# A late store in six parts instead of four, and the last store whole

## The chip, the cores and the metric

The kernel runs on one core of one Trainium2 chip. The metric is the device time of one execution in microseconds (us); the figure given for a kernel is the median of its runs.

## The reference

Eight batches of twelve heads, each with Q, K and V of 512 rows by 64 columns in float32. The softmax is over a 64 x 64 matrix of each head (attention between columns), and V is multiplied by it:

```python
Q_norm = Q / (np.linalg.norm(Q, axis=-2, keepdims=True) + 1e-10)
K_norm = K / (np.linalg.norm(K, axis=-2, keepdims=True) + 1e-10)
attn = np.einsum('bhnd,bhne->bhde', Q_norm, K_norm)
attn = np.exp(attn - np.max(attn, axis=-1, keepdims=True))
attn = attn / (np.sum(attn, axis=-1, keepdims=True) + 1e-10)
return np.einsum('bhnd,bhde->bhne', V, attn).astype(np.float32)
```

Q, K and V together are 37.75 MB to read, and the output is 12.58 MB to write.

## The kernel before

The 96 heads go in 24 units (`U`) of four heads, and two units make one of 12 steps (`S`). For a unit, Q and K are cast to bf16 side by side (`cast_qk`), and `grams` multiplies the pair by itself, so that one 128 x 128 matrix of a head holds the squares of the norms on its diagonal and Q against K off it. `squares`, `sums` and `powers` make the scales, `scale_k`, `logits`, `exps` and `normalise` the softmax, whose result stands as a block-diagonal `ab`. V goes in six groups (`W`): cast (`cast_v`), transposed on TensorE (`vtrans`), copied out of PSUM (`vcopy`) and multiplied by `ab` (`outs`). `ocopy` brings each of four outputs `x` of a step into an SBUF tile `so[s, i]`, two of them (halves of its rows) to a tile, and `store(s, i)` writes the tile to the output.

A tile `so[s, i]` has 128 partitions; in each lie two rows `r` of 2 KB, and the two rows go to different places of the output. A whole store is therefore 512 KB in 256 pieces of 2 KB. There are 24 stores, `(0, 0)` to `(11, 1)`, all issued from SP's queue. There are 13 `so` buffers.

The order of everything is worked out by a planner (`Order`): each piece of work has a cost on an engine, what must have ended before it, what it must follow, and a rank; for a store the rank is `v_at(...) + ST_LAG`, which puts most stores behind the loads. The planner's result is written out engine by engine. At the end of SP's queue stand, in this order, the rest of the loads, fourteen whole stores, the store `FEW = (S - 3, 1)`, which is `(9, 1)`, the stores `(10, 0)`, `(10, 1)`, `(11, 0)`, and the last one, `(11, 1)`, as two pieces of the planner, `sh` and `st`.

`store` treats two of these specially. For `FEW` it issues four DMAs: row 0 of partitions 0 to 91, of 92 to 95 and of 96 to 127 (L204), and then row 1 of all 128 partitions (L205). The two pieces of `(11, 1)` each take the half of the columns that one `ocopy` has written (`rows`, L207), so that a DMA has 256 pieces of 1 KB.

The DMAs use eight completion semaphores in turn: the one that is issued as the ninth has the semaphore of the first, and waits on SP until that first has landed in full.

Of the kernel before, what the change touches and what calls it, by code (L numbers as in the profile page):

```python
# [16 lines left out]
J = T // 2  # L17
# [85 lines left out]
def kernel(  # L103
# [7 lines left out]
    nc = tc.nc  # L111
# [3 lines left out]
    S = U // 2  # L115
# [46 lines left out]
    qk32, v32, vb, qkb, gram, scr, kq, n2, r8, kqs, rq, lg, ex, ab, vps, vt, po, so = ({} for _ in range(18))  # L162
# [32 lines left out]
        else:  # L195
            nc.sync.dma_start(out=o[:, c], in_=i[:, c])

    def store(s, i, k=None):
        rows = slice(None) if k is None else slice(k * (J // 2), (k + 1) * (J // 2))
        o = Of[s // 2, s % 2, i].rearrange("p r (j d) -> p r j d", d=D)  # L200
        if (s, i) == FEW:

            for a, b in ((0, 92), (92, 96), (96, 128)):
                nc.sync.dma_start(out=o[a:b, 0], in_=so[s, i][a:b, 0])  # L204
            nc.sync.dma_start(out=o[:, 1], in_=so[s, i][:, 1])  # L205
            return
        nc.sync.dma_start(out=o[:, :, rows], in_=so[s, i][:, :, rows])  # L207

    def cast_qk(u, x):
        s, r = divmod(u, 2)  # L210
# [137 lines left out]
    for i in range(NB["ab"]):  # L348
        a = const.tile([128, HU, 2 * D], BF16, name=f"ab{i}")
# [9 lines left out]
    X = 1.29  # L359
    R = dict(cq=2.5, gr=2.471, sq=0.756, kq=1, rd=3.457, pw=3.5, sc=1, rq=1.9, lg=5, ex=1.1, nm=2.545, cv=1.165, vt=0.9, vc=1.1, ou=2, oc=0.9)  # L360
    BIAS = dict(sc=-0.6, kq=5, cv=1, vc=-0.3, oc=0.6)
    QK_PACE, V_FROM, V_PACE, ST_LAG = 0.631, 0.0377, 0.7486, 1.5133

    def v_at(v):
        return V_FROM + V_PACE * v / U

    def piece(key, engines, after, behind, rank, fn, *args):
        if key[0] in ("cv", "vc", "oc", "kq", "sc"):
            plan.add(key, engines, after, behind, rank, lambda eng: fn(eng, *args))
        else:  # L370
            plan.add(key, engines, after, behind, rank, lambda eng: fn(*args))

    def back(kind, i, n, *rest):
        return (kind, i - n, *rest) if i - n >= 0 else None
# [17 lines left out]
    for u in range(U):  # L392
        s, r = divmod(u, 2)
# [17 lines left out]
    def turns(w):  # L411
        return [(q, f) for q in range(4) for f in ((0, 1) if w == W - 1 and q >= TAIL else (None,))]
# [29 lines left out]
    for s in range(S):  # L442
        for x in range(4):
            i, k = divmod(x, 2)
            n = 4 * s + x - 2
            wait = [("oc", n // 4, n % 4)] if n >= 0 else []
            order = [("ou", s, x - 1) if x else back("ou", s, 1, 3)]
            piece(("ou", s, x), {"PE": 0.5}, [("vc", s // 2, *t) for t in turns(s // 2) if t[0] // 2 == k] + [("nm", s)] + wait, order, R["ou"] + 0.01 * s, outs, s, x)
            n = 2 * s + i - NB["so"]
            free = [("st", n // 2, n % 2)] if k == 0 and n >= 0 else []  # L450
            order = [("oc", s, x - 1) if x else back("oc", s, 1, 3)]
            piece(("oc", s, x), {"ACT": 0.6, "DVE": (0.68, BIAS["oc"])} if s >= BOTH else {"ACT": 0.6}, [("ou", s, x)] + free, order, R["oc"] + 0.01 * s, ocopy, s, x)
        for i in range(2):
            order = [("st", s, 0) if i else back("st", s, 1, 1)]
            if (s, i) == (S - 1, 1):

                piece(("sh", s, i), {"DMA": 0.67}, [("oc", s, 2)], order, v_at(2 * s + i) + ST_LAG, store, s, i, 0)
                piece(("st", s, i), {"DMA": 0.67}, [("oc", s, 3)], [("sh", s, i)], v_at(2 * s + i) + ST_LAG, store, s, i, 1)
            else:
                piece(("st", s, i), {"DMA": X}, [("oc", s, 2 * i), ("oc", s, 2 * i + 1)], order, v_at(2 * s + i) + ST_LAG, store, s, i)  # L460

    ahead = [loaded(x, 0, r) for r in range(2) for x in range(2)]
    held, passed = [], False
# [40 lines left out]
```

## Time and profile before

| | us |
|---|---|
| median of 3 runs | 128.76 (128.62 to 128.79) |
| span of the profiled execution, first to last instruction | 127.0 |
| around the span, if that execution took the median time (no time of its own is listed for it) | 1.76 |
| DMA queue of SP (q1): share of 16 engines' span | 96.4% |
| DVE busy | 92.8 (73%) |
| TensorE busy | 77.7 (61%) |
| ACT busy | 72.5 (57%) |
| POOL busy | 36.6 (29%) |
| last copy into `so` (ACT, second of two from 114.00) ends | 115.1 |

A DMA runs on up to 16 DMA engines, and the profile's DMA share is the mean busy share of all 16; packets overlap a little, so that a share of 1.04 to 1.06 stands for all of them at work. "To landing" is the time from a DMA's issue until its semaphore has the last of its updates. The trace also records each update of a semaphore by a DMA, one for every DMA engine that carried a part of it: sixteen for most DMAs. These are called landings below. Times within the execution are in us from the start of its span.

### The profile page before, as it was taken

The numbers are of one execution on the slowest core, as the hardware profiler recorded it, in microseconds if no ns is written. First come the engines' busy times: TensorE is split into PE (matmuls) and PEld (weight loads), VectorE is DVE, ScalarE is ACT, GpSimd is POOL, SyncE is SP. The second block draws the span as 40 slices with busy tenths as digits, with TensorE's granted clock in tenths as the row PEclk, the third lists the DMA queues.
The fourth block names the chain that finished last, engine by engine and source line by source line (L and its number), as shares of the span: only waits on it lengthen the run. The fifth ranks groups of instructions, "written<-read, shape, count | busy, mean of one in ns | idle before, by whom it ended". The sixth has DMA issues, their size and how long they took to land.

```text
span 127.0 us, 4887 instructions
## 1 busy us (share of the span) xinstructions
PE 77.7 (61%) x2128; PEld 62.9 (50%) x2128; DVE 92.8 (73%) x141; ACT 72.5 (57%) x220; POOL 36.6 (29%) x40
## 2 busy tenths in 40 slices
PE   0065384894844679858594879566797869680000
PEld 0054372773633568647482668445585748460000
DVE  3354749859899899999885898999999799820000
ACT  4000441569877077786692786794829969972000
POOL 4006307300906903033065212213453361200000
PEclk9999999999998555999958967998559995955555
DMA  4999999999999999999999999999999999999993
GB/s 114 415 434 410 430 410 418 417 437 403 425 426 415 410 419 421 405 415 426 430 410 413 415 421 427 412 419 428 401 413 410 403 402 406 401 405 408 405 366 106
DMA packets 15629, 50.64 MB, mean 399 GB/s; under 512 B 1144, under 2 KB 1656, under 8 KB 14200
## 3 DMA queue, kind: packets, MB, share of 16 engines
q1 hardware_dynamic: 15320, 49.29, 96.4%
q10 hardware_dynamic: 288, 1.05, 2.1%
q8 instruction: 16, 0.26, 0.7%
q14 instruction: 5, 0.04, 0.1%
HBM read 37.75 MB, written 12.58 MB: 396 GB/s over the span
## 4 chain that ended last, share of the span: by engine, by line
DVE 39%; DMA 21%; PE 13%; ACT 11%; issue 4%; POOL 2%; DVEq 0%; SPq 0%; POOLq 0%; ACTq 0%
DMA qk<-in_Q_dram 21%; DVE qkb L213 15%; PE gram L233 9%; DVE scr L240 7%; DVE ab L291 6%; ACT vt L166 4%; DVE vb L168 4%; ACT ex L282 3%; ACT so L166 3%; PE vps L302 3%; DVE n L252 2%; DVE vt L168 2%; DVE so L168 2%; PE po L319 1%; ACT kq L166 1%
## 5 line engine op out<-in xcount | busy, mean ns | idle before, releaser
L233 PE MATMUL gram<-qkb 32*128 32x128 bf16 (+1 forms) x1504 | 35.5, 257 | 23.1 <-DVE qkb L213 9.9
L233 PEld LDWEIGHTS <-qkb 32*128 32x128 bf16 (+1 forms) x1504 | 29.9, 114 | 27.7 <-DVE qkb L213 12.7
L213 DVE CAST qkb<-qk 128x1024 bf16<-128x1024 f32 x48 | 36.4, 780 | 8.5 <-DMA qk<-in_Q_dram 6.9
L170 POOL TENSOR_SCALAR vb<-v 128x1024 bf16<-128x1024 f32 x19 | 21.2, 1129 | 45.5 <-DMA v<-in_V_dram 32.0
L166 ACT COPY so<-po 128x512 f32<-128x512 f32 x45 | 25.0, 593 | 5.2 <-PE po L319 5.0
L166 ACT COPY vt<-vps 128x1024 bf16<-128x1024 bf16 (+1 forms) x18 | 17.8, 989 | 17.4 <-PE vps L302 17.3
L302 PE MATMUL vps<-identb,vb 128*128 128x128 bf16 x192 | 20.2, 262 | 5.8 <-POOL vb L170 3.7
L319 PE MATMUL po<-ab,vt 128*64 128x128 bf16 x384 | 19.3, 242 | 5.2 <-issue 2.7
L263 POOL TENSOR_TENSOR kqs<-kq,r 64x512 f32<-64x512 f32 x12 | 14.0, 1164 | 25.8 <-ACT r L259 13.4
L240 DVE SCALAR_TENSOR_TENSOR scr<-gram,eye 64x512 f32<-64x512 f32 x24 | 16.5, 687 | 4.4 <-PE gram L233 4.1
L302 PEld LDWEIGHTS <-vb 128*128 128x128 bf16 x192 | 14.7, 117 | 10.0 <-POOL vb L170 5.1
L319 PEld LDWEIGHTS <-vt 128*64 128x64 bf16 x384 | 13.8, 121 | 9.2 <-issue 4.6
L282 ACT ACTIVATE ex<-lg,rq 128x64 f32<-128x64 f32 x48 | 14.5, 322 | 2.8 <-PE lg L276 2.7
L166 ACT COPY kq<-gram 64x512 f32<-64x512 f32 x12 | 7.0, 581 | 13.5 <-DVE scr L240 13.4
L291 DVE TENSOR_TENSOR ab<-ex,rinv 64x256 bf16<-64x256 f32 x24 | 13.9, 579 | 0.6
L282 ACT ACTIVATION_READ_ACCUMULATOR ex<-lg,rq 128x1 f32 x48 | 10.2, 213 | 0.0
L168 DVE CAST vb<-v 128x1024 bf16<-128x1024 f32 x5 | 7.6, 1527 | 1.2 <-DMA v<-in_V_dram 1.2
L252 DVE TENSOR_REDUCE n<-scr 128x8 f32<-128x512 f32 x12 | 8.1, 679 | 0.1
L276 PE MATMUL lg<-eye,kqs 64*128 64x64 f32 x48 | 6.4, 259 | 2.6 <-issue 1.5
L168 DVE COPY vt<-vps 128x1024 bf16<-128x1024 bf16 (+1 forms) x8 | 7.9, 1019 | 0.1
L276 PEld LDWEIGHTS lg<-eye,kqs 64*128 64x128 f32 x48 | 4.5, 156 | 4.4 <-issue 2.0
L288 DVE RECIPROCAL rinv<-esum 128x4 f32<-128x4 f32 x12 | 2.1, 171 | 2.8 <-ACT ex L282 2.8
(17 smaller groups left out, 16.0 us busy)
## 6 DMA issues: line engine op xcount, KB each, us to landing
v<-in_V_dram SPq DMA_DIRECT2D x11, 1024.0 KB, 17.1
out_dram<-so SPq DMA_DIRECT2D x22, 512.0 KB, 10.2
qk<-in_Q_dram SPq DMA_DIRECT2D x8, 1024.0 KB, 17.4
qk<-in_K_dram SPq DMA_DIRECT2D x8, 1024.0 KB, 17.1
qk<-in_Q_dram SPq DMA_DIRECT2D x8, 512.0 KB, 12.2
qk<-in_K_dram SPq DMA_DIRECT2D x6, 512.0 KB, 12.5
qk<-in_K_dram ACTq DMA_DIRECT2D x2, 512.0 KB, 7.3
v<-in_V_dram SPq DMA_DIRECT2D x2, 512.0 KB
```

The costliest lines, as they stand in the source:

```text
L166: nc.scalar.copy(o, i)
L168: nc.vector.tensor_copy(o, i)
L170: nc.gpsimd.tensor_scalar(out=o, in0=i, scalar1=1.0, scalar2=0.0, op0=ALU.mult, op1=ALU.add)
L213: nc.vector.tensor_copy(qkb[u][:, :, x * D:(x + 1) * D], qk32[s][:, x, r])
L233: nc.tensor.matmul(gram[s][:, h, r, 0], x, x, start=(t == 0), stop=(t == (T if u < WIDE else J) - 1))
L240: nc.vector.scalar_tensor_tensor(out=scr[s][half], in0=gram[s][half, :, :, 0, half].rearrange("p h r d -> p (h r) d"), scalar=1e-20, in1=e ...
L263: (nc.vector if eng == "DVE" else nc.gpsimd).tensor_tensor(out=kqs[s][HI], in0=kq[s][HI], in1=r8[s][HI, :, None].to_broadcast([D, 2 * HU, ...
L276: nc.tensor.transpose(l[:, h, :], kqs[s][HI, 2 * h:2 * h + 2].rearrange("p r d -> p (r d)"), eye2[HI])
L282: nc.scalar.activation(e[:, h, :], lg[s][:, h, :], AF.Exp, scale=rq[s][:, h:h + 1], accum_out=z[:, h:h + 1])
L291: nc.vector.tensor_tensor(out=a[half, :, half], in0=e[half], in1=ri[half, :, None].to_broadcast([D, HU, D]), op=ALU.mult,)
L302: nc.tensor.transpose(ps[:, c, n, :], vb[w][:, J * c + j].rearrange("p r d -> p (r d)"), identb)
L319: nc.tensor.matmul(po[s, x][e * D:(e + 1) * D, j].rearrange("p r d -> p (r d)"), v, ab[s][:, h, :])
```

## The change

Row 1 of the store `FEW` leaves in the same three parts as row 0, so that the store is six DMAs instead of four. The last store `(11, 1)` is one DMA with pieces of 2 KB instead of two with pieces of 1 KB, and the planner's special pieces for it go. The instructions of the other engines and their order are the same as before, and so is SP up to this store; SP has one DMA more in all (L204 six times, and L206 for the whole stores).

```diff
-    def store(s, i, k=None):
-        rows = slice(None) if k is None else slice(k * (J // 2), (k + 1) * (J // 2))
+    def store(s, i):
         o = Of[s // 2, s % 2, i].rearrange("p r (j d) -> p r j d", d=D)
         if (s, i) == FEW:
-            for a, b in ((0, 92), (92, 96), (96, 128)):
-                nc.sync.dma_start(out=o[a:b, 0], in_=so[s, i][a:b, 0])
-            nc.sync.dma_start(out=o[:, 1], in_=so[s, i][:, 1])
+            for r in range(2):
+                for a, b in ((0, 92), (92, 96), (96, 128)):
+                    nc.sync.dma_start(out=o[a:b, r], in_=so[s, i][a:b, r])
             return
-        nc.sync.dma_start(out=o[:, :, rows], in_=so[s, i][:, :, rows])
+        nc.sync.dma_start(out=o, in_=so[s, i])
...
-            if (s, i) == (S - 1, 1):
-                piece(("sh", s, i), {"DMA": 0.67}, [("oc", s, 2)], order, v_at(2 * s + i) + ST_LAG, store, s, i, 0)
-                piece(("st", s, i), {"DMA": 0.67}, [("oc", s, 3)], [("sh", s, i)], v_at(2 * s + i) + ST_LAG, store, s, i, 1)
-            else:
-                piece(("st", s, i), {"DMA": X}, [("oc", s, 2 * i), ("oc", s, 2 * i + 1)], order, v_at(2 * s + i) + ST_LAG, store, s, i)
+            piece(("st", s, i), {"DMA": X}, [("oc", s, 2 * i), ("oc", s, 2 * i + 1)], order, v_at(2 * s + i) + ST_LAG, store, s, i)
```

## The prediction

> **What bounds the kernel now.** First the table of stretches at the end of the span (columns: length, busy time of each engine, granted clock, DMA share of 16 engines, GB/s).
>
> ```profile
> 110.00:116.00 6.00, 3.32 (x62) 2.53 (x56) 1.71 (x4) 4.40 (x13) 0.00 (x0) 0.64 1.05 406
> 116.00:120.00 4.00, 0.00 (x0) 0.00 (x0) 0.00 (x0) 0.00 (x0) 0.00 (x0) 0.50 1.05 405
> 120.00:122.00 2.00, 0.00 (x0) 0.00 (x0) 0.00 (x0) 0.00 (x0) 0.00 (x0) 0.50 1.06 407
> 122.00:123.00 1.00, 0.00 (x0) 0.00 (x0) 0.00 (x0) 0.00 (x0) 0.00 (x0) 0.50 0.92 353
> 123.00:124.00 1.00, 0.00 (x0) 0.00 (x0) 0.00 (x0) 0.00 (x0) 0.00 (x0) 0.50 0.83 307
> 124.00:125.00 1.00, 0.00 (x0) 0.00 (x0) 0.00 (x0) 0.00 (x0) 0.00 (x0) 0.50 0.73 258
> 125.00:125.50 0.50, 0.00 (x0) 0.00 (x0) 0.00 (x0) 0.00 (x0) 0.00 (x0) 0.50 0.12 41
> 125.50:126.00 0.50, 0.00 (x0) 0.00 (x0) 0.00 (x0) 0.00 (x0) 0.00 (x0) 0.50 0.03 10
> 126.00:127.00 1.00, 0.00 (x0) 0.00 (x0) 0.00 (x0) 0.00 (x0) 0.00 (x0) 0.50 0.00 0
> ```
>
> After 116 no compute engine does anything. Only stores move, at 405 GB/s until 122, and then the rate falls in steps: DMA engines run out of work one after another. From 125.5 to 126 a share of 0.03 is 0.03 x 16 x 0.5 = 0.24 us of one engine's time: one engine alone is still at work. So the end is set by the DMA engine with most left to do, not by compute (the last copy into `so` ended at 115.1) and not by the mean of the engines.
>
> Next, SP's issues in time and what SP waited for (from 96 on): the stores are issued one by one as earlier ones land, eight back.
>
> ```profile
> 110.63 2.80 SPq L204 DMA_DIRECT2D out_dram<-so  x3
> 114.40 0.37 SPq L205 DMA_DIRECT2D out_dram<-so  x1
> 115.75 4.76 SPq L207 DMA_DIRECT2D out_dram<-so  x5
> ```
> ```profile
> SPq L207 <- DMA out_dram<-so: 6.8, 10, 0.9
> SPq L204 <- DMA out_dram<-so: 2.5, 3, 1.0
> ```
>
> Then the issues with their time to landing. The first four rows are of the store `FEW`, the last two of stretches that hold a whole store `(10, 0)` to `(11, 0)` and the first half of `(11, 1)`.
>
> ```profile
> out_dram<-so SPq DMA_DIRECT2D x1, 184.0 KB
> out_dram<-so SPq DMA_DIRECT2D x1, 8.0 KB
> out_dram<-so SPq DMA_DIRECT2D x1, 64.0 KB, 7.2
> out_dram<-so SPq DMA_DIRECT2D x1, 256.0 KB, 6.4
> ```
> ```profile
> out_dram<-so SPq DMA_DIRECT2D x1, 512.0 KB, 6.4
> out_dram<-so SPq DMA_DIRECT2D x1, 256.0 KB, 5.8
> ```
>
> The rows of 184 and 8 KB have no time to landing, and the landings tell why: each has four updates by DMA engines, where all others have sixteen. The part of 92 partitions landed at 118.70, 118.95, 119.30 and 119.94, that of 4 at 118.88, 119.12, 119.48 and 120.12: each 0.18 after the other, so the same four engines, which I call the four. The store before it landed on them at 116.85, 117.10, 117.44 and 118.09 (the four of its sixteen landings that the part of 92 follows by the same 1.85); 92 partitions on four engines are 23 pieces of 2 KB for each, 1.85 / 23 = 0.080 us a piece. Eight of the other twelve were late before it, at 119.11 to 119.52; four were early, 116.44 to 118.09. A whole store gives each engine 16 pieces, and the landings of two such follow at 1.27 to 1.30, again 0.080 a piece. The next DMAs keep the order: the slowest of the four is at 120.30 after the part of 32 partitions (113.1 + 7.2), 120.83 after the whole row (114.40 + 6.4), 122.12 after `(10, 0)` (115.75 + 6.4), then 123.41, 124.68, 125.37 (first half of the last store, 119.58 + 5.8) and 126.05, the last landing of all. The last half landed on the other fifteen at 122.48 to 125.54: 122.48, 122.69, 123.03 and 124.0 on the early four, the rest within 0.7 of each other. After 126.05 come 0.93 us of semaphore and drain work of the end.
>
> **The change part by part.**
> *Row 1 of `FEW` in three parts.* Before, each engine gets 8 pieces of it. After, each of the four gets 23 + 1 + 2 = 26 and each of the other twelve 2 (32 partitions over 16 engines). For the four that is 18 more: 18 x 0.080 = +1.45 us; for the twelve 6 fewer: -0.48 us. Price of the two extra DMAs on an engine: the slowest of the four had 1 + 2 + 8 pieces in three DMAs from 119.94 to 120.83, 0.89 / 11 = 0.081 a piece, so a DMA more costs next to nothing there (at most 11 x 0.001 = 0.01 us).
> *SP.* One DMA more in all, about 0.3 us of issue time (2.80 us are three of L204 and the waits between; the longest alone is 0.34), hidden, since SP is waiting between all of these. But each DMA takes one of the eight semaphores. The six parts wait for whole stores eight back, which landed at 110.57 and then every 1.28: issues at 110.6, 111.8, 113.1, 114.4, 115.7 and 117.0; `(10, 0)` at 118.25, 2.5 later than before, `(10, 1)` at 119.55, `(11, 0)` when the first part of 92 has landed (120.0), `(11, 1)` when the first part of 4 has (120.12) and SP is free (120.5). The four have work until after 122 and don't notice. The twelve have only 2 + 2 pieces between the store before `FEW` and `(10, 0)`. From issue to first packet it was 1.0 us at the start (Q's first load, issued 0.74, first packet 1.75), and at most 1.5 in this tail, where each next piece followed the last without a gap. So `(10, 0)` can start at 119.3 to 119.8. The eight late ones are through with the earlier pieces at 119.5 to 119.9: a gap of 0 to 0.3 us. The early four stand still for up to 1 us. This moves only engines with slack, as follows.
> *The last store whole.* Pieces of 2 KB in place of twice as many of 1 KB. Two halves took 0.69 + 0.69 on the slowest engine (124.68 to 126.05), a whole store 1.27 (123.41 to 124.68): -0.10 us on every engine. The wait for the last `ocopy` is no cost: it ended at 115.1, the issue is at 120.5, and the slowest engine gets to it at about 126.1. If that cover were gone, the cost would be the 0.5 us between the end of the two last copies; it is not.
> *Compute.* No instruction is moved on PE, DVE, ACT or POOL, and nobody waits for these stores: the tiles of `(9, 1)` to `(11, 1)` are not written again. Cost 0.
>
> **The sum.** Slowest of the four: 126.05 + 1.45 - 0.10 = 127.40. Slowest of the twelve: 125.54 - 0.48 - 0.10 + (0 to 0.3) = 125.0 to 125.3. The four are the last, so the end moves by 127.40 - 126.05 = +1.35 us. From the profiled span: 127.0 + 1.35 = 128.35. The median of the runs is 128.76, 1.76 over that span; with that unchanged, 130.1 us.
>
> One rule is to be weighed against these rows. The landings show four engines for the parts of 92 and 4 partitions. The Trainium skill, "DMA: Bandwidth & Descriptors", section "Why a DMA increments its semaphore by 16 and not by 1", has the number of engines as the largest up to 16 that divides the slowest dimension, and for such DMAs the lowest-numbered engines; 92 gives 4, as the trace has it, so the second part of 92 would meet the same four engines, and the sum is the +1.35 above. [...]
>
> **The rivals.** A measurement of this kernel can tell about 0.2% (0.26 us) from no change.
> *The four are not the last engines in an unprofiled run.* One trace shows that they are last, 126.05 against 125.54; the order could differ from run to run. If the slowest of the four is x us ahead of the slowest of the twelve, the gain is 0.58 on the twelve and the end moves by 1.35 - x, until x = 1.93. At x = 0.5: 129.6; at x = 1: 129.1. For: the page has 16 fetches of instructions with 0.7% of 16 engines' span, 0.007 x 16 x 127 / 16 = 0.9 us each, and one of them on another engine would change the order. Against: three runs within 0.17 us.
> *Faster:* the same with x over 1.93: the twelve decide, and -0.58 gives 128.2; it is faster by over 0.26 from x = 1.61 on. For: the twelve do shed 6 pieces each. Against: it needs a lag of over 2.1 us from what the trace shows.
> *The second part of 92 goes to other engines.* The early four could take +1.45 (their 124.0 becomes 125.4), and the first four would shed 0.58 (125.5): end 0.55 earlier, 128.2. If it took four of the late ones, 125.54 + 1.35 = 126.9, +0.85: 129.6. For: nothing names the engines in the landings. Against: the part of 4 met the very engines of the part of 92.
> *The queue runs dry.* With small parts in six of the eight places, the stores behind are issued 2.5 us later at most. It decides if the late ones of the twelve stand still for over 2.4 us (127.40 - 124.96). They are free at 119.9 at the latest and `(10, 0)` is issued at 118.25, so that takes over 4.1 us from issue to first packet; at 4.4 us the end is 0.3 later than in the sum, 130.4. Against: 1.0 to 1.5 in the trace.
>
> **How the numbers follow.** The sum as it stands, four last: 0.82, 129.9 to 130.3. The four ahead by less than 1.61: 0.08, 128.6 to 129.9, of which 0.02 within 0.26 of no change. Faster, by lead or by other engines: 0.05. Other engines and slower: 0.03; dry queue: 0.02. Faster 0.05, same 0.02, slower 0.93. The range takes the sum's own bounds, the first rival up to x = 0.6 (129.5) and the dry queue with the runs' scatter of 0.1 (130.5). Forecast 130.1.
>
> **What would show it.** Right: span 128.3 to 128.4; compute ends at the same 115; the stretch from 125.3 to 127.1 has a share of a quarter or less (four engines, one after another out of work); SP issues at the times above; two rows of 184 KB with four landings each; last landing near 127.4. Wrong: a last landing below 126.3, more than four engines at work after 125.5, or a stretch around 119 to 120 with a share far below 0.9 on which the end depends.

## The result and the profile after

The changed kernel takes 130.2 us (median of 4 runs, 129.99 to 130.32), the kernel before 128.72 us (4 runs, 128.62 to 128.79): a ratio of 1.0116, with a 95% interval of 1.0103 to 1.0129. The forecast was 130.1 us. The profiled execution took 130.32 us, 1.8 over its span of 128.5.

First the changed kernel's table of stretches at the end of the span (columns as before: length, busy time of each engine, granted clock, DMA share, GB/s).

```profile
116.00:118.00 2.00, 0.00 (x0) 0.00 (x0) 0.00 (x0) 0.00 (x0) 0.00 (x0) 1.00 0.90 349
118.00:119.00 1.00, 0.00 (x0) 0.00 (x0) 0.00 (x0) 0.00 (x0) 0.00 (x0) 0.53 0.84 320
119.00:120.00 1.00, 0.00 (x0) 0.00 (x0) 0.00 (x0) 0.00 (x0) 0.00 (x0) 0.50 0.84 322
120.00:122.00 2.00, 0.00 (x0) 0.00 (x0) 0.00 (x0) 0.00 (x0) 0.00 (x0) 0.50 1.05 407
124.00:125.00 1.00, 0.00 (x0) 0.00 (x0) 0.00 (x0) 0.00 (x0) 0.00 (x0) 0.50 0.84 326
125.00:125.50 0.50, 0.00 (x0) 0.00 (x0) 0.00 (x0) 0.00 (x0) 0.00 (x0) 0.50 0.28 111
125.50:126.00 0.50, 0.00 (x0) 0.00 (x0) 0.00 (x0) 0.00 (x0) 0.00 (x0) 0.50 0.23 90
126.00:126.50 0.50, 0.00 (x0) 0.00 (x0) 0.00 (x0) 0.00 (x0) 0.00 (x0) 0.50 0.15 57
126.50:127.00 0.50, 0.00 (x0) 0.00 (x0) 0.00 (x0) 0.00 (x0) 0.00 (x0) 0.50 0.09 33
127.00:127.50 0.50, 0.00 (x0) 0.00 (x0) 0.00 (x0) 0.00 (x0) 0.00 (x0) 0.50 0.02 8
```

Two things are new. At 125 the share falls to a quarter, which is four engines of sixteen, and these finish one after another until 127.2: the last packet ends at 127.17, and its landing follows 0.32 later, as in all traces here (0.32 to 0.34). And from 116 to 120 the share is below one: other engines stand still there, though their work is not done. Before, all sixteen were busy until 122.

SP's issues in time, then issues with their time to landing in the changed kernel (the 512 KB row is of the stretch around 118.6, the store `(10, 0)`; the others are of the whole span).

```profile
110.88 6.71 SPq L204 DMA_DIRECT2D out_dram<-so  x6
118.62 3.00 SPq L206 DMA_DIRECT2D out_dram<-so  x4
```
```profile
out_dram<-so SPq DMA_DIRECT2D x1, 512.0 KB, 5.0
out_dram<-so SPq DMA_DIRECT2D x2, 184.0 KB
out_dram<-so SPq DMA_DIRECT2D x2, 64.0 KB, 6.1
out_dram<-so SPq DMA_DIRECT2D x2, 8.0 KB
```

Both parts of 184 KB and both of 8 KB lack a time to landing, since each lands by four engines only. The landings of the second part of 92 are 120.84, 121.16, 121.62 and 122.10, those of the last store 125.03 to 125.28 on twelve engines and 126.23, 126.54, 127.00 and 127.49 on the four. `(10, 0)` is issued at 118.62 and lands on eight of the twelve between 121.17 and 121.26, nearly together: these had run out of work and began it together. The other four of the twelve follow by 121.44, 1.27 to 1.31 after their landings of the part before, so without a gap.

### The profile page after: what moved, and what is told of

Read it like the earlier page. It is cut to its first block, busy times and chain, and to the rows that moved or that the text cites. A ratio compares the mean times of both kernels' runs of the same rounds, so it can differ in the third digit from the quotient of the medians.

```text
span 128.5 us, 4887 instructions
## 1 busy us (share of the span) xinstructions
PE 78.1 (61%) x2128; PEld 63.7 (50%) x2128; DVE 93.5 (73%) x141; ACT 72.4 (56%) x220; POOL 36.2 (28%) x40
## 4 chain that ended last, share of the span: by engine, by line
DMA 55%; DVE 19%; PE 10%; ACT 2%; issue 2%; SPq 1%; ACTq 0%; DVEq 0%
DMA qk<-in_Q_dram 20%; DMA out_dram<-so 19%; DMA qk<-in_K_dram 15%; DVE qkb L212 7%; PE gram L232 6%; DVE scr L239 5%; DVE vt L168 3%; PE po L318 2%; DVE n L251 2%; DVE ab L290 2%; ACT so L166 1%; PE vps L301 1%; DVE so L168 1%; ACT ex L281 1%; PE lg L275 0%
## 5 line engine op out<-in xcount | busy, mean ns | idle before, releaser
L232 PE MATMUL gram<-qkb 32*128 32x128 bf16 (+1 forms) x1504 | 34.7, 253 | 22.8 <-DVE qkb L212 9.8
L232 PEld LDWEIGHTS <-qkb 32*128 32x128 bf16 (+1 forms) x1504 | 29.4, 113 | 27.1 <-DVE qkb L212 11.8
L318 PE MATMUL po<-ab,vt 128*64 128x128 bf16 x384 | 20.4, 253 | 6.0 <-DVE ab L290 2.2
L301 PE MATMUL vps<-identb,vb 128*128 128x128 bf16 x192 | 19.7, 259 | 5.9 <-POOL vb L170 3.8
L318 PEld LDWEIGHTS <-vt 128*64 128x64 bf16 x384 | 15.0, 129 | 10.0 <-issue 4.4
```

The lines of the kernel that those rows point to most:

```text
L232: nc.tensor.matmul(gram[s][:, h, r, 0], x, x, start=(t == 0), stop=(t == (T if u < WIDE else J) - 1))
L301: nc.tensor.transpose(ps[:, c, n, :], vb[w][:, J * c + j].rearrange("p r d -> p (r d)"), identb)
L318: nc.tensor.matmul(po[s, x][e * D:(e + 1) * D, j].rearrange("p r d -> p (r d)"), v, ab[s][:, h, :])
```

## The experiments

Ratios are to the kernel before, with their 95% intervals; its median beside these runs was 128.57 to 128.66 us.

**Each part of the change alone.** First the parts of row 1, with the last store still in halves (an edit of the kernel before):

```diff
-            for a, b in ((0, 92), (92, 96), (96, 128)):
-                nc.sync.dma_start(out=o[a:b, 0], in_=so[s, i][a:b, 0])
-            nc.sync.dma_start(out=o[:, 1], in_=so[s, i][:, 1])
+            for r in range(2):
+                for a, b in ((0, 92), (92, 96), (96, 128)):
+                    nc.sync.dma_start(out=o[a:b, r], in_=so[s, i][a:b, r])
```

> Row 1 of the store (9, 1) in parts of 92, 4 and 32; the last store still in two halves. Theory (four DMA engines carry 26 pieces of row 1 in place of 8, and they end last): 18 x 0.080 = +1.45 us on 128.72, 130.2 us; the slowest of the four lands at about 127.5. Rival (the parts cost nothing, the last store's shape does it): 128.7.

Measured: 130.1 us, 1.0108 (1.0095 to 1.0122), which is 1.45 over the 128.65 of the kernel before. The last landing is at 127.33. The parts of row 1 carry the whole loss.

Then the last store whole, with `FEW` as in the kernel before (an edit of the changed kernel, the reverse of the diff above):

> The last store whole, the store (9, 1) as before. Theory (two halves of 1 KB pieces take 0.69 + 0.69 us on an engine, a whole store 1.28): -0.10 us, 128.6 us. Rival (the halves let the queue go on earlier, so that joining them costs): +0.1 or more, 128.8 and up.

Measured: 128.42 us, 0.9981 (0.9971 to 0.9991), a small gain. The size is 0.23 by the medians, where 0.10 was expected; a later pair of runs goes into this.

**The number of DMAs against the number of engines.** Row 1 goes in three parts again, at the same places of the queue, but in parts that spread over 8, 12 and 16 engines:

```diff
-            for r in range(2):
-                for a, b in ((0, 92), (92, 96), (96, 128)):
+            for r, ends in enumerate(((0, 92, 96, 128), (0, 8, 32, 128))):
+                for a, b in zip(ends, ends[1:]):
                     nc.sync.dma_start(out=o[a:b, r], in_=so[s, i][a:b, r])
```

> As the changed kernel, but row 1 of the store (9, 1) goes in parts of 8, 24 and 96 partitions, which spread over 8, 12 and 16 engines: 9, 8 or 6 pieces for an engine in place of 8. The number of DMAs, their place in the queue and the waits for semaphores are those of the changed kernel. Theory of the four engines: the four have 1 piece more (+0.08) and -0.10 of the last store, 128.7 us. Rival (the number of DMAs, or eight places in the queue taken by small parts): 130.1 as for the changed kernel. The landings also show which engines are among the lowest eight and twelve.

Measured: 128.75 us, 1.0008 (0.9998 to 1.0017). Six DMAs for the store and six of eight places in the queue filled with small parts cost nothing that stands out; the rival falls. The stretches of this kernel show that engines do run dry here too, without moving the end, and that no data is moved after 125.5. The last landing, 125.89, is of the slowest of the four, 0.41 after the next:

```profile
116.00:118.00 2.00, 0.00 (x0) 0.00 (x0) 0.00 (x0) 0.53 (x1) 0.00 (x0) 0.50 0.93 357
125.00:125.50 0.50, 0.00 (x0) 0.00 (x0) 0.00 (x0) 0.00 (x0) 0.00 (x0) 0.50 0.08 29
125.50:126.00 0.50, 0.00 (x0) 0.00 (x0) 0.00 (x0) 0.00 (x0) 0.00 (x0) 0.50 0.00 0
```

The part of 8 partitions lands by eight engines, that of 24 by twelve. The four of the part of 4 are among the eight: 119.05, 119.34, 119.72 and 120.31, each 0.35 to 0.37 after that engine's landing of the part of 4 (118.68, 118.99, 119.35, 119.95). So a part on fewer engines falls on a subset of those of a wider part.

**The size of the part.** Row 1 in parts of 76, 4 and 48 partitions, otherwise the changed kernel:

```diff
-            for r in range(2):
-                for a, b in ((0, 92), (92, 96), (96, 128)):
+            for r, ends in enumerate(((0, 92, 96, 128), (0, 76, 80, 128))):
+                for a, b in zip(ends, ends[1:]):
```

> As the changed kernel, but row 1 of the store (9, 1) goes in parts of 76, 4 and 48 partitions: 19 + 1 + 3 = 23 pieces for each of the four engines, 15 more than before. Theory (the cost goes with the pieces of the four): 15 x 0.080 - 0.10 = +1.10 us, 129.8 us. Rival (a cost for each split, whatever the sizes): 130.2 as the changed kernel.

Measured: 129.84 us, 1.0087 (1.0071 to 1.0102). The last landing is at 127.04, against 127.49 in the changed kernel; the slowest of the four passed the first part of 92 at 119.81 and 120.02, so 0.24 of the 0.45 are the three pieces fewer and 0.21 an earlier start. The cost follows the pieces on the four.

**No narrow part at all.** Both rows of `(9, 1)` whole, and the last store whole:

```diff
-            for r in range(2):
-                for a, b in ((0, 92), (92, 96), (96, 128)):
+            for r, ends in enumerate(((0, 128), (0, 128))):
+                for a, b in zip(ends, ends[1:]):
```

> The store (9, 1) in two whole rows, no part of 92 at all, and the last store whole. Theory (the end is that of the engine with most left): against the kernel with only the last store whole (128.42), the four shed 18 pieces of row 0 and the other twelve take 6 more each, 6 x 0.080 = +0.48. The slowest of the twelve was level with the four to 0.5 us ahead of them, so the twelve now decide: 0 to +0.5 us, 128.4 to 128.9 us, with the four about 1.4 us ahead of the last. Rival (every DMA that is split costs by itself): faster than 128.4.

Measured: 128.85 us, 1.0021 (1.0007 to 1.0036): 0.4 to 0.5 over the kernel with only the last store whole, by the ratios. Of that, 0.12 is not the engines but work after the last landing (0.96 us here, 0.84 there; the next section says why). The narrow parts of row 0 are worth keeping. The stretches show the other side of the balance:

```profile
123.00:124.00 1.00, 0.00 (x0) 0.00 (x0) 0.00 (x0) 0.00 (x0) 0.00 (x0) 0.50 0.69 268
124.00:125.00 1.00, 0.00 (x0) 0.00 (x0) 0.00 (x0) 0.00 (x0) 0.00 (x0) 0.50 0.55 213
125.00:125.50 0.50, 0.00 (x0) 0.00 (x0) 0.00 (x0) 0.00 (x0) 0.00 (x0) 0.50 0.44 168
```

Half of the engines are through at 124.5 (landings of the last store: eight at 122.94 to 124.53), and the other eight finish together at 125.71 to 125.95. In the changed kernel only four were left at 125.

**A smaller part in row 0.** The four with a little less, row 1 and the last store whole, first parts of 76, 4 and 48 (shown), then of 68, 12 and 48 (`(0, 68, 80, 128)`):

```diff
-            for r in range(2):
-                for a, b in ((0, 92), (92, 96), (96, 128)):
+            for r, ends in enumerate(((0, 76, 80, 128), (0, 128))):
+                for a, b in zip(ends, ends[1:]):
```

> As the kernel with only the last store whole, but row 0 of (9, 1) goes in parts of 76, 4 and 48 partitions: 23 pieces for each of the four in place of 26, 3 for the others in place of 2. Theory: the four -0.24, the twelve +0.08: by the trace of before, where the four were 0.5 us later than the rest, -0.24 (128.2 us), by that of the kernel with the last store whole, where they were level, 0 (128.4 us).

> The same with row 0 in parts of 68, 12 and 48: 21 pieces for each of the four, 4 for the next eight engines, 3 for the last four. Theory: the four -0.40, eight of the others +0.16: -0.35 us by the trace of before (128.1 us), +0.1 by that of the kernel with the last store whole (128.5 us).

Measured: 128.41 us, 0.9983 (0.9969 to 0.9997), and 128.33 us, 0.9983 (0.9970 to 0.9997). Both beat the kernel before by about 0.2%, and neither can be told from the kernel with only the last store whole (0.9981). With the last landing at 125.83 and 125.56, and eight or nine of the engines within half a microsecond of it, little is left there; what is left is three engines other than the four that end at 122.6 to 123.2, and no part tried puts work on those alone.

**The same parts early.** Row 0 of `(9, 1)` in its parts as before, the last store whole, and the narrow parts of row 1 moved to the store `(1, 0)`, which is issued among the loads:

```diff
+        if (s, i) == (1, 0):
+            for r, ends in enumerate(((0, 128), (0, 92, 96, 128))):
+                for a, b in zip(ends, ends[1:]):
+                    nc.sync.dma_start(out=o[a:b, r], in_=so[s, i][a:b, r])
+            return
```

> As the kernel with only the last store whole (128.42), and row 1 of a much earlier store, (1, 0), issued among the loads, goes in parts of 92, 4 and 32; row 1 of (9, 1) is whole. Theory (an engine's total counts, since the queue is never empty): the four end 18 x 0.080 = 1.45 us later again, about 129.8 us. Rival (only a late split counts, since an early one is evened out before the end): 128.4 to 128.7.

Measured: 130.34 us, 1.0133 (1.0109 to 1.0157). That is 0.5 over the expectation; the next section adds it up. Early or late, the loss is the same size or more; that the split store is late does not matter. The end looks like that of the changed kernel, with four engines alone:

```profile
125.50:126.00 0.50, 0.00 (x0) 0.00 (x0) 0.00 (x0) 0.00 (x0) 0.00 (x0) 0.50 0.24 94
126.50:127.00 0.50, 0.00 (x0) 0.00 (x0) 0.00 (x0) 0.00 (x0) 0.00 (x0) 0.50 0.09 33
127.00:127.50 0.50, 0.00 (x0) 0.00 (x0) 0.00 (x0) 0.00 (x0) 0.00 (x0) 0.50 0.02 8
```

**What a store in halves costs.** The last four stores each in halves, with `FEW` as before, beside the kernel with only the last store whole, run again:

```diff
+        if s >= S - 2:
+            for k in range(2):
+                rows = slice(k * (J // 2), (k + 1) * (J // 2))
+                nc.sync.dma_start(out=o[:, :, rows], in_=so[s, i][:, :, rows])
+            return
```

> The store (9, 1) as before, and each of the last four stores, not the last alone, in two halves of 1 KB pieces. The last store whole was worth 0.23 us by the medians (interval of the ratio 0.9971 to 0.9991), where the pieces on an engine gave 0.10. Theory (each store in halves costs every engine 0.10 us): four times 0.10 over the kernel with the last store whole, 128.8 us. Rival (a store in halves costs 0.23 by something that the engines' pace does not show): four times 0.23, 129.3 us.

> The kernel with the last store alone whole again, on the same chip as the one with four stores in halves: 128.4 to 128.6 us, 0.1 to 0.2 under the kernel before.

Measured: 129.09 us, 1.0035 (1.0022 to 1.0049), and 128.52 us, 0.9986 (0.9976 to 0.9996). The difference is 0.57, or 0.14 for a store, between the two expectations and nearer to 0.10 (0.40 for four) than to 0.23 (0.92). In the traces the slowest engine takes 5.47 us for the four stores in halves (120.93 to 126.40) and 5.14 for four whole ones (120.62 to 125.76): 0.08 a store, 0.33 for four. The rest lies behind the last landing: 1.10 us of work there against 0.84 with whole stores (the next section says why), 0.25 more. The two make up the 0.57. So the rival was right that something beside the engines' pace counts, though not in its size, and it is not a cost of each half. The gain of the one store made whole divides likewise: 0.10 of pace and 0.10 behind the last landing (0.94 in the kernel before, 0.84), where the two pairs of runs gave 0.23 and 0.14.

## Why the prediction was right

*The bound.* Forecast: the four engines with most left set the end. The last landing is theirs at 127.49, forecast 127.40. With the same number of DMAs on more engines the loss is gone, with 15 extra pieces in place of 18 it is smaller, and at another place in the queue it is there again. Compute ended at 115.6, 0.5 later than before; that is still far ahead of the stores.

*Eighteen pieces more at 0.080.* From the first part of 92 to the last landing the slowest of the four needs 127.49 - 120.02 = 7.47 us for 93 pieces, 0.080 each. Of the 0.09 by which the forecast missed the last landing, 0.08 is an earlier difference: that engine passed its first part at 120.02, not 119.94.

*The twelve.* Forecast for the slowest of them: last landing at 125.0 to 125.3, measured 125.28. The other eleven are within 0.25 of it, because most of them had to wait for `(10, 0)` and began it together.

*The dry queue.* Forecast: `(10, 0)` issued at 118.25 and started 1.0 to 1.5 later, a standstill of 0 to 0.3 us on the late ones and up to 1 on the early four. It was issued at 118.62 (the waits began 0.3 late in this execution) and landed first at 121.17. Less 0.32 from last packet to landing and 16 pieces (1.28), it began at 119.57, 0.95 after its issue, about as at the start of the kernel (1.0). The prediction compared first packets with landings here, which come 0.32 later. The standstill of the late ones fits all the same: landing by landing it is up to 0.3 (119.59 for the part before, 121.17 - 1.28 = 119.89 for the start).

The early four stood still for longer than forecast. The second part of 32 waited for its semaphore as well and was issued at 117.27, when three of them had landed the first at 116.67 to 117.18. So they were idle twice, and the earliest had two pieces to move from 116.4 to 119.6: about 3 us of standstill, not 1. This is the share of 0.90 and 0.84 between 116 and 120. It cost nothing, as these engines had more slack than that: they land their last store with the rest of the twelve, 2.2 us before the end. The rival's condition of a 2.4 us standstill of the late ones was far off.

*The last store whole.* Forecast -0.10 on every engine. The traces of the changed kernel (1.27 for the last store) and of the parts alone (0.68 + 0.68) have 0.09, the four stores in halves 0.08 each. Sign and size were right; what the runs gave beyond it lies behind the last landing.

*The first rival.* With `FEW` as in the kernel before, the slowest of the four was never ahead of the rest: 0.5 us behind in its trace, and 0.1 behind in the two with only the last store whole. That they are nearly level would explain why the kernel gains so little from more balance. By its own sum this rival's times begin at 128.5 (1.35 - 1.61 = -0.26), not at 128.6.

*Behind the last landing.* The prediction took the 0.93 us there as fixed. It is not. SP closes the kernel by waiting for the completion semaphores, two to an instruction and always in the same order, and each of these that finds its semaphores complete adds 0.06 us. The eight semaphores are used in turn, so the number of DMAs decides which one the last store has, and with it how many waits still follow:

| kernel | closing waits that still follow | last landing to end, us |
|---|---|---|
| only the last store whole (two executions); smaller part in row 0 (two kernels) | 0 | 0.83 to 0.84 |
| before; both rows whole | 2 | 0.94; 0.96 |
| changed; row 1 in parts of 8, 24, 96; of 76, 4, 48 | 3 | 1.01 |
| parts of row 1 alone; the same parts early | 4 | 1.08 |
| four stores in halves | 4 | 1.10 |

For the changed kernel it is +0.08, beside +1.45 and -0.10: together 1.43, measured 1.48.

*What stays open.* Against the kernel with only the last store whole, the changed kernel is 1.7 us slower by the ratios (1.0116 against 0.9981 and 0.9986); the eighteen pieces and the closing waits make 1.45 + 0.17 = 1.62. The early split is 1.9 to 2.0 slower, where 1.45 + 0.24 = 1.69; the rest is within the interval of its ratio (0.3 us to either side). In eight executions of seven kernels that do not differ before it, the slowest of the four passes the first part of 92 at 119.72 to 120.05. Whether these 0.3 us are scatter or have a cause the runs do not settle.

## What to carry to other kernels

Where a kernel ends on a queue of transfers, look at how many DMA engines are still at work in the last microseconds, not at the mean GB/s: the end is that of the one engine with most pieces left. A transfer with a partition count such as 92 goes to few engines, and every piece counted on those, early or late, is added to the end once they are the last. Such a part can level engines that lag unequally, but only up to the point where they are level; a second one of the same kind costs its full size. Before reading a difference of a tenth of a microsecond, take off the work after the last landing: here it changed with the number of DMAs alone.

## What the runs showed of the hardware

Parts of 92, 76, 68 and 4 partitions each landed by four engines, of 8 by eight, of 12 and 24 by twelve, of 32, 48, 96 and 128 by sixteen. (Each of those on fewer than sixteen shows one update more, 0.1 to 0.2 us after its issue ended and at least 1 us before its first landing; it is not counted.) The rule of the Trainium skill that the prediction used ("DMA: Bandwidth & Descriptors", section "Why a DMA increments its semaphore by 16 and not by 1") gives just these numbers, as the largest divisor up to 16; that they are the lowest-numbered engines is not to be seen in the landings, only that a narrow part's engines are among those of a wider one. A piece of 2 KB took an engine 0.080 us and one of 1 KB 0.043 (0.68 for 16), alone or beside fifteen others. A landing came 0.32 to 0.34 us after the last packet, and a closing wait on complete semaphores took SP 0.06 us. Not expected: before `(9, 1)`, in all the kernels here whose earlier stores are whole, the engines fall into two groups, some seven or eight of them 1 to 3 us ahead of the rest, and the four are in the leading group. So the first narrow parts on them only use up a lead. Why these lead is not shown by any run.
